# A one-layer hybrid trunk: the recurrent chain's operands kept as one DRAM record per chunk, causal mask and softmax normalisation moved

## The chip, the cores and the metric

The kernel runs on one core of a Trainium2 chip. The metric is device time in microseconds (us) of one execution. It is compared with a reference in float32.

## The reference, cut to what matters

One layer of a parallel-branch block works on T = 528 tokens (16 learned meta tokens ahead of 512) of width 1024. One input projection feeds a recurrent branch (RWKV-7, 8 heads of 64), an attention branch with forget gates (FoX, 8 heads of 64) and two sets of gates; the output of the meta tokens is dropped at the end.

```
u = rmsnorm(h);  proj = u @ w_in
# recurrent branch, per head, token by token:
sa = S a_t;  S = S * w_t + sa b_t + v_t k_t;  y_t = S r_t
y = groupnorm(y);  y_rw = (y + bonus) * g
# attention branch, per head, causal, in blocks of 128 queries:
logits = q k^T * scale + (F_q - F_k)
p = softmax(where(kpos <= qpos, logits, -inf));  y_fx = p v
# merge and MLP
h += (sig(gA) * (y_rw @ w_out_rw) + sig(gB) * (y_fx @ w_out_fx)) @ w_o
h += square(relu(rmsnorm(h) @ w_up)) @ w_down
```

## The kernel before, in words

**Features.** Every large product is made in three passes: each operand is split into a high and a low fp32r part, and hi-hi, lo-hi and hi-lo products are added up. The input projection (L468, tile `pj`) is 480 such weight blocks of 128x128, 1,440 matmuls: 24 feature jobs (12 for the recurrent branch, 12 for attention, each in two halves of 264 tokens) and 16 gate jobs of 512 tokens. Gates (`gt`) are stored to DRAM (`gd`, L491) and fetched again (`gl`, L1056) for the out projection.

**The recurrent branch** works in 4 pairs of heads (class `Pair`). For a pair, `decay` (L686; its first product is `pup`, L698) makes the decays, `keys` the keys (`BK` holds two key forms, L732), `rows` (L736) the decayed rows `L[e]` for each head e of the pair, in nine chunks of 64 tokens, `scores` (L763) the products of keys and rows (`psr`, L773) times a triangular mask. One head's products fill 128 partitions of PSUM, of which 64 go masked into `Bm` (L776) and 64 into the empty half of `L[e]` (L777), so that there are two multiplies for each of 24 PSUM tiles. `keys_turned` (L779) makes `bkT` (`pbt`, L788), `inverse` (L792) inverts the triangular matrices of a group of two pairs into `Tt`, and `chain` (L884) then steps through nine chunks for the group g = 0 or 1. A chunk is four dependent products: `pch` from `uv` and `L` (L911), a copy `Rs` (L913), `pch` from `Rs` and `Tt` (L917), two copies into `uv` (L919), the new state from `uv` and `bkT` (L932, L934), and the output `pyy` (L940, L943). The values of the next chunk are transposed inside the chain (`pvt`, L897) and copied into `uv` (L899). After chunks 4 and 8 `group_norm` (L951) normalises the output: DVE works out y (L954 to L963, with a Newton iteration for the reciprocal root, L221 to L228), PE transposes it (`pyt`, L970), adds the bonus `bv` and multiplies by the gate product `pg` (L977). All of this stays in SBUF: `L`, `Bm`, `bkT`, `ov` and `bv` are held for two pairs at a time. Pair 2 therefore waits for the first chain (`chained`, `normalised`, `values_read`, `inverted`) before it writes them.

**Attention** has 4 pairs with 4 query blocks i each (`attention`, L571): scores `psc` (L592), the causal mask added on DVE (L601), a fused add of the decay and running minimum (`pe`, `nm`, L603), an exponential with its sum on ACT (L606), a reciprocal (`rsum`, L607) and the division of the whole row by the sum on DVE (L608), transposes to `ppt`/`ppm` (L621, L623), copies (L625, L626), the product with the values `py` (L634, L637) in two 64-column halves of the array, one for each head, and a copy into `y_fx` (L638).

**What sets the order.** TensorE (PE) runs its instructions in the order in which they are written, and a planner writes them. `Clock` (L60) books an estimated duration for every instruction and keeps the time at which each tile is written and read. `Turns` (L150) has streams with a rank; it takes the stream of lowest rank whose next step is ready on the planner's clock with a margin (ROOM). Ranks: chain 0, recurrent 1, attention 2, attention's features 3, group norm 4, projections 8. So the projections are what fills PE between steps of the others. The other engines' instructions are sorted by a scheduler after the planner's urgency. All DMAs are issued in order by one queue, SP. PSUM has 8 banks: `pj` 2, the small products 4, `py` 1, `ch` 1.

After the mixer come the out projection (L1063) with the gates fetched again, merged on POOL (L1057, L1067), the product with w_o (L1095, L1112), a norm, and the MLP (L1146 up, L1179 down).

Of the kernel before, what the change touches and what calls it, by code (L numbers as in the profile page):

```python
# [12 lines left out]
I32 = mybir.dt.int32  # L13
# [46 lines left out]
class Clock:  # L60
# [13 lines left out]

    def last(self, name):
        return max(self.w.get(name, 0.0), self.r.get(name, 0.0))
# [6 lines left out]
    def ready(self, *aps):  # L83
        return max([self.w.get(a.tensor.name, 0.0) for a in aps] + [0.0])
# [11 lines left out]
    def read(self):  # L96
# [3 lines left out]
        for x in new:  # L100
# [10 lines left out]
            names = [a.tensor.name for a in ins]  # L111
# [5 lines left out]
            deps = max([self.w.get(n, 0.0) for n in names] + [self.free.get(out, 0.0)])  # L117
            if eng == "PE":
                n = max(cols(outs[0]), 64)
                big = tuple(x.tile_size) == (128, 128)  # L120
                if ins[0].dtype == F32R:
# [7 lines left out]
            else:  # L129
                size = max([cols(a) for a in outs + (ins if "Reduce" in str(x.opcode) else [])])  # L130
                if eng in self.RATE:
                    fixed, per = self.RATE[eng]

                    if eng == "DVE" and not any(a.tensor.space == PSUM for a in ins + outs):
                        fixed += 0.2
                    end = self.book(eng, max(deps, self.last(out)), fixed + per * size) + fixed + per * size
                else:
                    cost = 0.3 + size * 128 * 4 / 2.0e5
                    end = self.book("DMA", max(deps, self.last(out)), cost) + cost + 2.0
            for o in outs:  # L140
                self.w[o.tensor.name] = max(self.w.get(o.tensor.name, 0.0), end + self.HOP)
            for n in names:
                self.r[n] = max(self.r.get(n, 0.0), end + self.HOP)
# [6 lines left out]
class Turns:  # L150
# [4 lines left out]
    ROOM = {0: 0.0, 1: 0.8, 2: 1.5, 3: 1.5, 4: 2.5, 8: 0.5}  # L155
# [9 lines left out]
    def run(self):  # L165
        ck = self.clock
        while self.streams:
# [10 lines left out]
            ck.urgent = s[0] < 2  # L178
            with self.tc.high_priority() if ck.urgent else nullcontext():
# [8 lines left out]
def kernel(ctx, tc, ht, x, win, par, cst, gain, lora, wout, wo, wup, wdn, out, dbg=None):  # L188
# [15 lines left out]
    cs = cp.tile([128, 576], F32, name="cs")  # L204
    pr = cp.tile([128, N_PAR], F32, name="pr")
    ident, ones_blk, tmask, cmask = (cs[:, 128 * i:128 * i + 128] for i in range(4))
    mask16 = cs[:, 512:]
# [5 lines left out]
    qg8 = cp.tile([128, 1], F32, name="qg8")  # L213
    eps = cp.tile([128, 1], F32, name="eps")
    smask = cp.tile([128, NCH, 64], BF16, name="smask")

    def rsqrt(x, pool, tag, shape, iters=3):

        y = pool.tile(shape, F32, name=tag + "y", tag=tag + "y")
        w = pool.tile(shape, F32, name=tag + "w", tag=tag + "w")  # L220
        V.tensor_scalar(y.bitcast(I32), x.bitcast(I32), -0.5, float(0x5F3759DF), ALU.mult, ALU.add)  # L221
        c = 1.0
        for _ in range(iters):
            V.tensor_tensor(w, x, y, ALU.mult)
            V.tensor_tensor(w, w, y, ALU.mult)
            V.scalar_tensor_tensor(y, w, 3.0 * c * c, y, ALU.subtract, ALU.mult)
            c = -2.0 * c ** 3
        V.tensor_scalar(y, y, 1.0 / c, None, ALU.mult)  # L228
        return y
# [37 lines left out]
    yp = ctx.enter_context(tc.tile_pool(name="yp", bufs=1))  # L267
    gates_d = [dr.tile([128, S], F32, name=f"gd{i}") for i in range(16)]

    with ExitStack() as st:  # L270
# [38 lines left out]
        V.memset(eps, 1e-6)  # L309
        nc.scalar.preload_act_table_set("natural_log_exp_and_others")  # L310
# [7 lines left out]
        with tc.tile_pool(name="xp", bufs=2) as xp:  # L318
# [16 lines left out]
            nc.sync.dma_start(cs, cst)  # L335
# [3 lines left out]
            shifts = [tshift(12 + blk, lfs[i], name="tl", tag="ov", bufs=2) for i, blk in enumerate((B_LORA, B_GD))]  # L339
            for t in range(2):  # L340
# [28 lines left out]
                V.tensor_tensor(f0[:, tk], pf, rs[:8, tk], ALU.mult)  # L369
        y_rw = yp.tile([128, 4, S], F32, name="y_rw")  # L370
# [35 lines left out]
        for t_ in (lhi, llo):  # L406
            ck.w[t_.tensor.name] = 10.0
# [36 lines left out]
        def projections(total):  # L444
            fetched, done = None, 0
            while done < total:
# [5 lines left out]
                while cur is not None:  # L452
# [6 lines left out]
                    for a0, a1 in parts:  # L459
# [16 lines left out]
                        ck.urgent = rank < 2  # L476
                        if finish:
                            with tc.high_priority() if ck.urgent else nullcontext():
                                finish()
                        ck.read()  # L480
                        ck.urgent = False
# [18 lines left out]
        def fox_features():  # L500
            for p in range(4):
# [57 lines left out]
                vm = fp.tile([48, 128], F32, name="vm", bufs=2)  # L559
# [6 lines left out]
                for e, hs in enumerate(hss):  # L566
                    A.copy(vm[32 * e:32 * e + 16, hs], pvm[:16, hs])
# [3 lines left out]
        def attention():  # L571
            for p in range(4):
# [10 lines left out]
                def scored(i):  # L583
# [5 lines left out]
                    for a, b in parts:  # L589
                        for e, hs in enumerate(hss):  # L590
                            sc = psm("psc")[:, :b - a]
                            mm(sc, q[hs, 128 * i:128 * i + 128], k[hs, a:b], start=True, stop=True)  # L592
                            scs[e].append((sc, a, b))
                    pes = []
                    for e in range(2):
# [3 lines left out]
                        for x, (sc, a, b) in enumerate(scs[e]):  # L599
                            if b == n:  # L600
                                V.tensor_tensor(sc[:, b - a - 128:], sc[:, b - a - 128:], cmask, ALU.add)  # L601
# [3 lines left out]
                        rsum = fp.tile([128, 1], F32, name="rsum", bufs=3)  # L605
                        act(pe[:, :n], pe[:, :n], AF.Exp, bias=least, scale=-1.0, accum_out=rsum)  # L606
                        V.reciprocal(rsum, rsum)  # L607
                        V.tensor_scalar(pe[:, :n], pe[:, :n], rsum, None, ALU.mult)  # L608
                        pes.append(pe)
                    return pes  # L610

                def turned(i, pes):

                    pTs = []
                    pTm = fp.tile([48, 128], F32, name="pTm")
                    for e in range(2):
                        pe, m = pes[e], slice(32 * e, 32 * e + 16)
# [8 lines left out]
                        A.copy(pTm[m], ptm)  # L626
# [635 lines left out]
```

## Time and profile before

| | |
|---|---|
| median of 3 runs | 959.02 us (956.32 to 959.78) |
| the profiled execution | 958.41 us, its span 956.4 us |
| PE busy | 892.9 us, 93% of the span |
| DVE busy | 508.6 us, 53% |
| ACT busy | 438.9 us, 46% |
| POOL busy | 193.4 us, 20% |
| mean granted TensorE clock | 0.957 |
| DMA | 83.30 MB, mean 87 GB/s |

The times of one execution start at zero with the first instruction; 2.0 us of its time lie outside the span. In the views an instruction is named by its line, operation and tiles, output first ("pch<-uv,L"); "x8" means eight in a row taken together; brackets give the idle time of the engine ahead of it and the instruction that ended it. PEclk is the granted TensorE clock as a share of full speed. A float32 product that is not a transpose appears as two matmul records. SPq is the DMA queue's own sequencer.

### The profile page before, as it was taken

Reading aid. Unit: us, or ns where it says so; the run is one execution under the profiler, and the core shown is the slowest. Engines: PE = TensorE matmul, PEld = TensorE weight load, DVE = VectorE, ACT = ScalarE, POOL = GpSimd, SP = SyncE. Lnnn points to the kernel's source line nnn. Section 1 sums busy time; section 2 is a strip of 40 time slices with the busy share of each in tenths; the row PEclk is TensorE's granted clock in tenths of the full one; section 3 lists DMA queues with packets and bytes.
Section 4 is the critical chain, followed back from the end, with each engine's and each line's share of the span. In section 5 each row is a group of like instructions: output and inputs, shape, how many; then the busy total and the mean of one; then the engine's idle time right before and its main releaser. Section 6 shows DMA issues by size and latency. Waiting matters only on the chain.

```text
span 956.4 us, 15455 instructions
## 1 busy us (share of the span) xinstructions
PE 892.9 (93%) x5968; PEld 725.9 (76%) x5968; DVE 508.6 (53%) x1013; ACT 438.9 (46%) x899; POOL 193.4 (20%) x169
## 2 busy tenths in 40 slices
PE   7789998989979997999979799999999999999998
PEld 6667866758878765877558578988888888888886
DVE  6584677344767588354765655454523245543332
ACT  7745535675627545375644444343422224442221
POOL 1352643212524342421015510000000000000000
PEclk9887989999979999999979979999999999999999
DMA  5210213123101231311254452033333233333331
GB/s 200 86 59 24 67 56 108 36 67 100 48 30 49 67 103 48 111 35 46 67 169 150 157 158 72 2 108 91 97 99 99 92 96 99 100 99 93 116 121 56
DMA packets 45449, 83.30 MB, mean 87 GB/s; under 512 B 5048, under 2 KB 6200, under 8 KB 45376
## 3 DMA queue, kind: packets, MB, share of 16 engines
q1 hardware_dynamic: 45376, 82.32, 27.7%
q8 instruction: 47, 0.77, 0.3%
q14 instruction: 26, 0.21, 0.1%
HBM read 75.99 MB, written 6.31 MB: 86 GB/s over the span
## 4 chain that ended last, share of the span: by engine, by line
PE 62%; DVE 8%; ACT 5%; POOL 3%; DMA 2%; issue 1%; POOLq 0%; DVEq 0%; ACTq 0%; SPq 0%
PE po L1146 18%; PE pd L1179 18%; PE pj L468 11%; PE po L1095 2%; PE po L1112 2%; DMA gl<-gd 2%; POOL gl L1057 1%; PE py L637 1%; POOL gl L1067 1%; PE psc L592 1%; DVE tmp L824 1%; PE pw L842 1%; ACT L256 1%; PE ppt L623 1%; PE pch L917 1%
## 5 line engine op out<-in xcount | busy, mean ns | idle before, releaser
L238 DVE TENSOR_TENSOR wlo<-wraw,whi 128x512 fp32r<-128x512 f32 x152 | 109.4, 721 | 184.5 <-ACT whi L237 183.0
L237 ACT CAST whi<-wraw 128x512 fp32r<-128x512 f32 x152 | 94.0, 620 | 196.1 <-PE pd L1179 109.6
L468 PE MATMUL pj<-uhi,whi 128*128 128x264 f32 (+1 forms) x480 | 171.0, 356 | 0.2 <-ACT qa L519 0.2
L468 PE MATMUL pj<-uhi,wlo 128*128 128x264 f32 (+1 forms) x480 | 158.9, 331 | 0.5 <-POOL wlo L440 0.5
L468 PE MATMUL pj<-ulo,whi 128*128 128x264 f32 (+1 forms) x480 | 159.1, 331 | 0.0
L440 POOL TENSOR_TENSOR wlo<-wraw,whi 128x512 fp32r<-128x512 f32 x80 | 107.9, 1355 | 217.6 <-ACT whi L439 201.3
L468 PEld LDWEIGHTS pj<-uhi,whi 128*128 128x128 f32 x480 | 94.5, 197 | 20.5 <-issue 10.6
L468 PEld LDWEIGHTS pj<-uhi,wlo 128*128 128x128 f32 x480 | 94.8, 198 | 8.2 <-POOL wlo L440 0.7
L1179 PE MATMUL pd<-whi,fhi 128*128 128x512 f32 x256 | 99.6, 389 | 0.0
L1179 PE MATMUL pd<-wlo,fhi 128*128 128x512 f32 x256 | 99.6, 389 | 0.0
L1179 PE MATMUL pd<-whi,flo 128*128 128x512 f32 x256 | 99.6, 389 | 0.0
L468 PEld LDWEIGHTS pj<-ulo,whi 128*128 128x128 f32 x480 | 95.1, 198 | 4.8
L1146 PE MATMUL po<-zhi,whi 128*128 128x512 f32 (+1 forms) x248 | 94.8, 382 | 0.0
L1146 PE MATMUL po<-zlo,whi 128*128 128x512 f32 (+1 forms) x248 | 94.8, 382 | 0.0
L1146 PE MATMUL po<-zhi,wlo 128*128 128x512 f32 (+1 forms) x248 | 94.8, 382 | 0.0
L439 ACT CAST whi<-wraw 128x512 fp32r<-128x512 f32 x80 | 48.9, 617 | 44.6 <-PE pj L468 25.3
L1179 PEld LDWEIGHTS pd<-wlo,fhi 128*128 128x128 f32 x256 | 48.1, 188 | 10.0
L1179 PEld LDWEIGHTS pd<-whi,fhi 128*128 128x128 f32 x256 | 48.1, 188 | 9.9
L1179 PEld LDWEIGHTS pd<-whi,flo 128*128 128x128 f32 x256 | 48.1, 188 | 9.9
L1146 PEld LDWEIGHTS po<-zhi,wlo 128*128 128x128 f32 x248 | 46.6, 188 | 9.1
L1146 PEld LDWEIGHTS po<-zlo,whi 128*128 128x128 f32 x248 | 46.6, 188 | 9.1
L1146 PEld LDWEIGHTS po<-zhi,whi 128*128 128x128 f32 x248 | 46.6, 188 | 8.9
(303 smaller groups left out, 1509.5 us busy)
## 6 DMA issues: line engine op xcount, KB each, us to landing
wraw<-in_win SPq DMA_DIRECT2D x84, 256.0 KB, 2.8
wraw<-in_wup SPq DMA_DIRECT2D x64, 256.0 KB, 2.6
wraw<-in_wdn SPq DMA_DIRECT2D x64, 256.0 KB, 2.6
gd<-gt SPq DMA_DIRECT2D x16, 256.0 KB, 2.1
wraw<-in_wout SPq DMA_DIRECT2D x16, 256.0 KB, 2.8
gl<-gd SPq DMA_DIRECT2D x16, 256.0 KB, 3.0
wraw<-in_wo SPq DMA_DIRECT2D x16, 256.0 KB, 3.0
xt<-in_ht SPq DMA_DIRECT2D x8, 264.0 KB, 5.8
```

The lines of the kernel that those rows point to most:

```text
L237: A.copy(hi, raw)
L238: low.tensor_tensor(lo, raw, hi.bitcast(F32), ALU.subtract)
L256: p = nc.scalar.preload_act_table_set("natural_log_exp_and_others")
L439: A.copy(hi, raw)
L440: G.tensor_tensor(lo, raw, hi.bitcast(F32), ALU.subtract)
L468: mm(po, a, b[:, k, a0:a1], start=n == 0, stop=n == 23)
L592: mm(sc, q[hs, 128 * i:128 * i + 128], k[hs, a:b], start=True, stop=True)
L623: nc.tensor.transpose(pt[:, 128 * j:128 * j + 128], pe[:, NM + 128 * j:NM + 128 * j + 128], ident)
L1095: mm(pd[i], a[:, k, 128 * i:128 * i + 128], b, start=k == 0 and n == 0, stop=k == 7 and n == 2)
L1112: mm(po, a[:, k, 128 * i:128 * i + 128], b[:, k, :], start=n == 0, stop=n == 23)
L1146: mm(po[:, t0:t1], a, b[:, k, t0:t1], start=n == 0, stop=n == 23)
L1179: mm(pd[i], a[:, b_, 128 * i:128 * i + 128], b, start=b_ == 0 and n == 0, stop=b_ == 15 and n == 2)
```

## The change

**Records.** What the chain needs of a pair is written to DRAM, one record of 128x512 floats for each chunk: both heads' rows with their masked scores (columns 0 to 255), `bkT` (256 to 383), the second part of the masked scores (384 to 447) and `Tt` (448 to 511). `save` stores a part as soon as it is made. Values are transposed beforehand (`values_turned`) and stored in `vt_d`, the bonus in `bv_d`. The chain fetches two records and two halves of `uv` for the next chunk at the start of each one; `uv` has 2 buffers and `rec` 4. The waits of pair 2 for the first chain go, and only the second chain waits for the first one's last group norm.

**Scores and rows.** The masked scores of a head go with one multiply into one tile M[e]; rows for both heads are made together on 128 partitions.

**Attention.** The mask is added by a product of two bf16 tiles in PSUM. The exponentials are transposed and multiplied undivided; in `mixed` the exponentials are now the stationary operand, with all 128 columns, and the values the moving one; the result is scaled by the reciprocal sum on ACT, and transposed back on PE.

**Group norm** takes ln and exp on ACT for the reciprocal root. One of the two copies into `uv` (L919) is on ACT.

**Planner.** The clock keeps regions of tiles in place of whole tiles, and DMA costs by length of run. Ranks are now chain 0, attention 1, attention's features 2, recurrent 3.

```diff
-    ROOM = {0: 0.0, 1: 0.8, 2: 1.5, 3: 1.5, 4: 2.5, 8: 0.5}
+    AHEAD = {0: 100, 1: 40, 2: 20, 3: 20}
+    ROOM = {0: 0.0, 1: 1.0, 2: 1.5, 3: 1.0, 4: 2.5, 8: 0.5}
...
+    rec_d = [dr.tile([NCH, 128, 512], F32, name=f"rec{i}") for i in range(4)]
+    vt_d = [dr.tile([NCH, 64, 2, 2, 64], F32, name=f"vtd{i}") for i in range(2)]
+    bv_d = [dr.tile([128, S], F32, name=f"bvd{i}") for i in range(4)]
...
-                            mm(sc, q[hs, 128 * i:128 * i + 128], k[hs, a:b], start=True, stop=True)
+                            mm(sc, q[hs, 128 * i:128 * i + 128], k[hs, a:b], start=True, stop=b < n)
+                    for e in range(2):
+                        mm(scs[e][-1][0][:, b - a - 128:], masks[:, 0, :], masks[:, 1, :], start=False, stop=True)
...
-                            if b == n:
-                                V.tensor_tensor(sc[:, b - a - 128:], sc[:, b - a - 128:], cmask, ALU.add)
...
-                        V.tensor_scalar(pe[:, :n], pe[:, :n], rsum, None, ALU.mult)
...
-                    for j in range(i + 1):
-                        for e, hs in enumerate(hss):
-                            mm(py[hs], vt[:, j, hs], pTs[e][0][:, j, :], start=False, stop=j == i)
-                    A.copy(y_fx[:, p, 128 * i:128 * i + 128], py)
+                        mm(py[:, hs], pTs[e][1], vm[:, hs], start=True, stop=False)
+                        for j in range(i + 1):
+                            mm(py[:, hs], pTs[e][0][:, j, :], vt[:, j, hs], start=False, stop=j == i)
+                    yn = fp.tile([128, 128], F32, name="yn")
+                    for e, hs in enumerate(hss):
+                        act(yn[:, hs], py[:, hs], AF.Copy, scale=sums[e])
+                    yield lambda: max(ck.ready(yn), banks(1))
+                    pyT = psm("pyT")[:, :128]
+                    nc.tensor.transpose(pyT, yn, ident)
+                    A.copy(y_fx[:, p, 128 * i:128 * i + 128], pyT)
...
+            def save(self, rows, c0, c1, src):
+
+                nc.sync.dma_start(rec_d[self.p][:, rows, c0:c1].rearrange("c q x -> q c x"), src)
...
-                    for e, hs in enumerate(hss):
-                        os, sp = hss[1 - e], sps[e]
-                        V.tensor_tensor(Bm[hs, c0:c0 + 3, :], sp[hs, :3, :], bc(tmask[hs], 1, 3), ALU.mult)
-                        V.tensor_tensor(L[e][os, c0:c0 + 3, :], sp[os, :3, :], bc(tmask[os], 1, 3), ALU.mult)
+                    for e in range(2):
+                        V.tensor_tensor(M[e][:, c0:c0 + 3, :], sps[e][:, :3, :], bc(tmask, 1, 3), ALU.mult)
+
+                for e, hs in enumerate(hss):
+                    self.save(hss[1 - e], 128 * e, 128 * e + 128, M[e][hss[1 - e]])
+                    self.save(hs, 384, 448, M[e][hs, :, 64:])
...
+            def fetch_rec(c):
+                recs = []
+                for q in prs:
+                    t = rp.tile([128, 512], F32, name="rec", bufs=4)
+                    nc.sync.dma_start(t, rec_d[q.p][c])
+                    recs.append(t)
+                return recs
...
             for c in range(NCH):
-                yield lambda: ck.ready(uv)
+                nxt = None
+                if c < NCH - 1:
+                    nxt, nxt_recs = new_uv(c + 1), fetch_rec(c + 1)
+                yield lambda: ck.ready(uv, *recs)
...
-                for e, hs in enumerate(hss):
-                    V.tensor_copy(uv[hs, 0, e], ch[hs, 1])
+                for e, (hs, copy) in enumerate(zip(hss, (V.tensor_copy, A.copy))):
+                    copy(uv[hs, 0, e], ch[hs, 1])
...
-            rs = rsqrt(st2, rp, "rsg", [128, 2, 4])
-            V.tensor_tensor(y, y, bc(rs, 3, 64), ALU.mult)
+            after(act(st2, st2, AF.Ln, bias=epsg, scale=1.0 / 64), pinned(s_))
+            act(st2, st2, AF.Exp, scale=-0.5)
+            V.tensor_tensor(y, y, bc(st2, 3, 64), ALU.mult)
...
-        turns.add(1, recurrent())
-        turns.add(2, attention())
-        turns.add(3, fox_features())
+        turns.add(3, recurrent())
+        turns.add(1, attention())
+        turns.add(2, fox_features())
```

How the order moves is shown at three places. The first is PE near the end of the mixer. Before, this is what stands behind the last projection matmul (`pj`); the streams named are the second chain (`pch`), attention of pair 3 (`ppt`) and the group norm (`pyt`, `pg`).

```order
L468 MATMUL pj<-uhi,wlo 128x512
L917 MATMUL pch<-Rs,Tt 64x64 x4
L897 MATMUL pvt<-cs,ov 64x128 x2
L621 MATMUL ppt<-cs,pe 16x128
L623 MATMUL ppt<-cs,pe 128x128
L970 MATMUL pyt<-cs,y_rw 64x128 x4
L977 MATMUL pg<-lhi,lw_4541 128x256
L977 MATMUL pg<-llo,lw_4541 128x256
L977 MATMUL pg<-lhi,lw_4542 128x256
L932 MATMUL pch<-uv,bkT 64x64 x4
```

And this is what stands around the last projection matmul now.

```order
L653 MATMUL ppt<-cs,pe 16x128
L655 MATMUL ppt<-cs,pe 128x128 x3
L500 MATMUL pj<-uhi,whi 128x512
L500 MATMUL pj<-ulo,whi 128x512
L500 MATMUL pj<-uhi,wlo 128x512
L1021 MATMUL pyt<-cs,y_rw 64x128 x4
L1028 MATMUL pg<-lhi,lw_4667 128x256
L1028 MATMUL pg<-llo,lw_4667 128x256
L1028 MATMUL pg<-lhi,lw_4668 128x256
L625 MATMUL psc<-ka,qa 128x272 x2
L625 MATMUL psc<-ka,qa 128x256 x2
```

Before, the whole last chunk of the chain and query blocks 1 to 3 of pair 3 stand behind the last `pj`; now the chain has ended ahead of it, and of attention only the scores of query block 3 and what follows them stand behind it. The number of `pj` matmuls is the same, 1,440. From the first to the last chunk's first product the first chain had 189 of them before and has 63 now (the place of 36 of the former is taken by steps of pair 2 and of attention); the second chain had 132 and has 102. At the start of PE's order 36 `pj` stood ahead of the first `pup`, and 78 do now.

The second place is the DMA queue SP while the first chain runs. Before, it holds weights (`wraw`, `lraw`) and a gate's store.

```order
L658 DMA lraw<-in_lora 128x128 [waits DVE_49,PE_49]
L430 DMA wraw<-in_win 128x512 [waits DMAHW3_49,Pool_49]
L658 DMA lraw<-in_lora 128x128 [waits DMAHW2_49,DMAHW0_49,DVE_49]
L430 DMA wraw<-in_win 128x512 [waits DMAHW7_49]
L491 DMA gd_77<-gt 128x512 [waits Activation_49]
L658 DMA lraw<-in_lora 128x128 [waits DMAHW5_49,DMAHW2_49,DVE_49]
L430 DMA wraw<-in_win 128x512 [waits DMAHW6_49,Pool_49]
```

Now the chain's fetches stand in it: `rec` is a pair's record, `uv` the values, `vtd` their store; `rec_77<-M` is a save of pair 2.

```order
L940 DMA rec<-rec_75 128x512 [waits DMAHW4_49,PE_49]
L948 DMA uv<-vtd_79 64x2x128 [waits DMAHW5_49,DMAHW6_49,PE_49,Activation_49]
L948 DMA uv<-vtd_79 64x2x128
L940 DMA rec<-rec_76 128x512 [waits DMAHW7_49]
L462 DMA wraw<-in_win 128x512 [waits DMAHW0_49]
L521 DMA gd_90<-gt 128x512 [waits DMAHW1_49,Activation_49]
L802 DMA rec_77<-M_2569 64x9x128 [waits DMAHW2_49,DVE_49]
L948 DMA uv<-vtd_79 64x2x128 [waits DMAHW3_49,PE_49]
```

Each chunk has four fetches, the first of which wait for PE (the products that read the buffers two chunks back), and a gate's store and a save stand among them. The whole queue holds 452 rows in place of 309.

The third place is SP where the out projection begins. Before, the residual `hres` stands ahead of the gates `gl`:

```order
L234 DMA wraw<-in_wout 128x512 [waits DMAHW2_49,DVE_49,Activation_49]
L1076 DMA hres<-in_x 128x1024 [waits DVE_49,PE_49,Activation_49]
L1076 DMA hres<-in_x 128x1024 x3
L1056 DMA gl_5588<-gd_75 128x512 [waits DVE_49,PE_49,DMAHW3_49,Activation_49,Pool_49]
L1056 DMA gl_5606<-gd_83 128x512 [waits DMAHW4_49]
```

Now the gates come first:

```order
L256 DMA wraw<-in_wout 128x512 [waits DMAHW6_49,DVE_49,Activation_49]
L1097 DMA gl_5719<-gd_85 128x512 [waits DMAHW0_49,DVE_49,Activation_49]
L1097 DMA gl_5737<-gd_93 128x512
L1097 DMA gl_5770<-gd_86 128x512
L1097 DMA gl_5788<-gd_94 128x512 [waits DMAHW7_49]
```

The first `gl` waited for PE and POOL before, and does not wait for them now.

More of the change, by code (lines that the diff above doesn't have):

```diff
@@ L135, in read @@
                         fixed += 0.2
-                    end = self.book(eng, max(deps, self.last(out)), fixed + per * size) + fixed + per * size
+                    end = self.book(eng, deps, fixed + per * size) + fixed + per * size
                 else:
[L138 to L143, printed above, removed]
+                    run = min(self.run(a) for a in outs + ins)
+                    cost = 0.1 + 4 * math.prod(n for _, n in outs[0].ap) / (1.2e5 if run < 128 else 2.0e5 if run < 512 else 3.3e5)
+                    end = self.book("DMA", deps, cost) + cost + 2.0
+            for g in go:
+                self.note(self.w, *g, end + self.HOP)
+            for g in gi:
+                self.note(self.r, *g, end + self.HOP)
 class Event:
@@ L475, in projections @@
                         ck.read()
[L476 removed]
+                        ck.urgent = False
                         if finish:
[L478 removed]
+                            with tc.high_priority(20) if rank < 9 else nullcontext():
                                 finish()
[L480 to L481 removed]
                     ev.done = True
@@ L840, in six @@
                 for n in range(b0, b0 + 6):
-                    for hs in hss:
-                        mm(ps_[hs, n - b0, :], lhs(n)[hs], rhs(n)[hs], start=True, stop=True)
-                return ps_
-            def now(t):
-                ck.read()
-                return ck.ready(t)
-            at = now(Dn)
-            w2_at, d_at, w_at = [], [], []
+                    for e, hs in enumerate(hss):
+                        mm(ps_[hs, n - b0, :], lhs(n, e)[hs], rhs(n)[hs], start=True, stop=True)
@@ new lines, in recurrent @@
+            for p, q in enumerate(pairs):
+                g, j = divmod(p, 2)
+                yield from q.decay()
+                yield q.k_in
+                yield from q.keys()
+                done = Event()
+                if j == 0:
+                    pairs[p + 1].ask_keys(done)
+                yield q.r_in
+                q.rows()
+                done.done = True
+                yield from q.scores()
+                yield from q.keys_turned()
+                yield q.v_in
+                yield from q.values_turned()
+                yield from q.bonus()
+                if p < 3:
+                    pairs[p + 1].ask_values()
+                if j == 1:
+                    if g == 0:
+                        pairs[2].ask_keys()
+                    yield from inverse(g, pairs[p - 1:p + 1])
+                    turns.add(0, chain(g, pairs[p - 1:p + 1]))
```

270 lines of the change are left out of this document (131 added, 139 removed).

## The prediction

> **What bounds the kernel now.** I read the busy times by stage first. Columns: window, its length, busy time of PE, PE's weight loads, DVE, ACT and POOL with their instructions, granted clock, DMA share, GB/s.
>
> ```profile
> 28.00:464.00 436.00, 398.67 (x3598) 320.50 (x3598) 268.37 (x596) 239.59 (x531) 153.29 (x134) 0.94 0.20 61
> 464.00:497.00 33.00, 24.36 (x194) 16.84 (x194) 26.49 (x85) 17.63 (x49) 0.00 (x0) 0.76 0.38 128
> 602.00:956.00 354.00, 350.38 (x1617) 292.83 (x1615) 138.44 (x205) 113.04 (x190) 0.00 (x0) 1.00 0.31 93
> ```
>
> The MLP (602 on) keeps PE busy for 350.4 of 354 us at full clock, and no edit touches it. The change lies in the mixer, 28 to 497. PE is busy there for 398.7 + 24.4 = 423 of 469 us, so 46 us are idle; and the clock, 0.94 over 436 us and 0.76 over 33, costs up to 26 + 8 = 34 us more, as far as PE worked meanwhile. Everything that the change can win is in these 80 us. Next, who ends PE's idle time in the mixer: total us, times, longest.
>
> ```profile
> PE psr L773 <- DVE L L777: 7.4, 4, 4.2
> PE pup L698 <- ACT lhi L261: 5.9, 1, 5.9
> PE psr L773 <- DVE BK L732: 5.6, 2, 3.8
> PE ppt L621 <- DVE rsum L607: 5.5, 1, 5.5
> PE pyt L970 <- DVE y_rw L963: 4.7, 1, 4.7
> ...
> PE ppm L621 <- DVE pe L608: 2.3, 1, 2.3
> PE psr L773 <- DVE nm L603: 2.2, 1, 2.2
> ```
>
> These seven are 33.6 of the 46 us: DVE late with the masked scores and with the softmax, a group norm, and one stall at the start. None is a DMA. The clock I read in three stretches of 10 us:
>
> ```profile
> 70.00:80.00 10.00, 9.90 (x48) 7.58 (x46) 6.67 (x14) 3.56 (x6) 2.49 (x2) 0.50 0.19 52
> 120.00:130.00 10.00, 8.37 (x41) 6.62 (x41) 8.53 (x15) 1.44 (x4) 4.17 (x5) 0.66 0.18 54
> 270.00:280.00 10.00, 7.75 (x40) 6.93 (x41) 9.53 (x26) 0.54 (x2) 0.20 (x1) 0.50 0.08 28
> ```
>
> The clock falls to half behind a long wait and stays there for some 10 us: a stall costs about its length again.
>
> **The end of the mixer.** Start, time over the row's matmuls, and in brackets PE's wait:
>
> ```profile
> 463.57 0.40 PE L468 MATMUL pj<-uhi,wlo 128*128 128x512 f32 x1
> ...
> 470.47 0.45 PE L943 MATMUL pyy<-uv,Bm 64*64 64x64 f32 x8
> ...
> 481.75 1.03 PE L970 MATMUL pyt<-cs,y_rw 128*64 128x128 f32 x4 [4.72 <-DVE y_rw L963]
> ...
> 485.60 1.59 PE L592 MATMUL psc<-ka,qa 64*128 64x272 f32 x6
> ...
> 488.36 0.88 PE L637 MATMUL py<-pT,vt 128*64 128x128 f32 x12
> 491.54 0.38 PE L621 MATMUL ppm<-cs,pe 128*16 128x128 f32 x1 [2.31 <-DVE pe L608]
> ...
> 497.08 0.80 PE L1063 MATMUL po<-yhi,whi 128*128 128x512 f32 x1 [0.36 <-ACT y_fx L638]
> ```
>
> The last filler ends near 464, the chain at 470.9. The 26.2 us from there to the out projection (497.1) hold the window's 8.6 us of idle time (33 - 24.4); of the other 17.6, some 7 are lost to the clock (33 x 0.24 = 8 in the window from 464), which leaves 10.6 of work at full clock. So 15.6 us are lost.
>
> **The change part by part**, against the profiled execution's 958.41 us (2.0 us outside its span of 956.4), which is 0.6 us under the median.
>
> *1. End.* By the new order 33 more projection matmuls stand beside attention's blocks 0 to 2 and the chain has ended before the last of them. Bare are only the scores of block 3 with what follows, the piece from 485.60 to 497.08, 11.5 us, of which by the same share (10.6 of 26.2, a little more because its rows are dense) 5.2 are work. The division (L608) goes from that path, but a scaling on ACT, a transpose and one more copy come in, so I leave 11.5. That is 6.3 us lost in place of 15.6: **-9** (0 to -13).
>
> *2. Start.*
>
> ```profile
> 31.78 0.28 PE L468 MATMUL pj<-uhi,wlo 128*128 128x264 f32 x1
> 37.96 0.59 PE L698 MATMUL pup<-lhi,lw 64*128 64x264 f32 x2 [5.89 <-ACT lhi L261]
> ```
>
> Now 78 `pj` stand ahead of this product and not 36. The 42 more take 42 x 0.12 = 5.0 us (the rows ahead of 31.78 follow each other at 0.12), nearly all of the wait: **-5** (-3 to -6). If ACT is later than now, behind the table load and copy that it has there in the new order, the rest remains.
>
> *3. DVE's waits.* What DVE loses, us in all and mean ns:
>
> ```profile
> L608 DVE TENSOR_SCALAR pe<-pe,rsum 128x144 f32<-128x144 f32 (+3 forms) x32 | 15.0, 474 | 0.6
> ...
> L776 DVE TENSOR_TENSOR Bm<-psr,cs 64x384 f32<-64x384 f32 x24 | 13.2, 549 | 0.8 <-PE psr L773 0.6
> L777 DVE TENSOR_TENSOR L<-psr,cs 64x384 f32<-64x384 f32 x24 | 13.1, 554 | 0.4
> ...
> L743 DVE TENSOR_SCALAR L<-okk 64x9 f32<-64x9 f32 x8 | 9.0, 1128 | 0.0
> L601 DVE TENSOR_TENSOR psc<-psc,cs 128x128 f32<-128x128 f32 x32 | 8.9, 294 | 5.1 <-PE psc L592 5.0
> ```
>
> L608 and L601 go (23.9), one of each pair L776/L777 goes (13.1), L743 is halved (4.5): 41 of DVE's 268.4 + 26.5 = 295 us, without the smaller ones. In the score waits a bank comes free after one multiply of 0.55 us and not two; in the softmax waits 0.47 + 0.29 us go for each head. These waits (7.4 + 5.6 + 2.2 + 5.5 + 2.3 = 23.0) should about halve: **-12** (-4 to -18). `BK` (5.6) gets no faster itself, only less queued.
>
> *4. Clock.* Of the 26 us in 28 to 464, the stretches behind waits of 3.8 us and more are what (2) and (3) can mend. I take two of some 5 us each, 10 us at 0.50: **-10** (-3 to -20).
>
> The Trainium skill, "TensorE: Matmul & The Clock Gate", section "Part 1: The HAM clock gate", has the array at half rate after at least one idle window of about 3.4 us and at full rate after one busy window. By that rule waits that merely shrink below 3.4 us would already save their whole stretch, and the term would be -15 and the sum 935. The stretch 120 to 130, at 0.66, speaks against so sharp an edge, since no wait near it is long:
>
> ```profile
> 116.12 0.46 PE L773 MATMUL psr<-L,BK 64*128 64x128 f32 x2 [1.75 <-DVE BK L732]
> 120.47 0.46 PE L773 MATMUL psr<-L,BK 64*128 64x128 f32 x2 [1.21 <-DVE L L777]
> 122.09 1.10 PE L773 MATMUL psr<-L,BK 64*128 64x128 f32 x10 [1.16 <-DVE L L777]
> ```
>
> Several waits of 1.2 to 1.8 us within 8 us are enough here. So I stay with -10.
>
> *5. More work on PE.* The old `py` products use two 64-column halves side by side: at 488.36 twelve records start within 0.88 - 0.27 us, 0.055 each. On the whole array the nearest row is a 128x128 product with 128 weight columns:
>
> ```profile
> 458.06 0.60 PE L562 MATMUL pv<-cs,vf 128*128 128x128 f32 x4
> ```
>
> Here four start within 0.60 - 0.27 us, 0.109 each. The new `mixed` has 112 products in 224 records: 224 x (0.109 - 0.055) = 12.1. The 32 mask products are bf16 and unseen: 0.05 to 0.11 each, 2.6 in the middle; 16 transposes at 0.109 make 1.7. Fewer changes between halves and whole array give back some 2. Sum **+14** (+8 to +20). PE is the bound wherever filler stands, so this counts in full.
>
> *6. Fetches of the chain.* Now 72 DMAs stand on its path, in order on SP. The nearest rows (KB, then us to landing) and the chain's period:
>
> ```profile
> gd<-gt SPq DMA_DIRECT2D x16, 256.0 KB, 2.1
> ...
> gl<-gd SPq DMA_DIRECT2D x16, 256.0 KB, 3.0
> ```
>
> ```profile
> 496.87 1.75 SPq L1056 DMA_DIRECT2D gl<-gd  x4
> ```
>
> ```profile
> 443.21 0.45 PE L911 MATMUL pch<-uv,L 128*64 128x64 f32 x8
> ...
> 447.32 0.45 PE L943 MATMUL pyy<-uv,Bm 64*64 64x64 f32 x8
> ...
> 449.37 0.45 PE L911 MATMUL pch<-uv,L 128*64 128x64 f32 x8
> ```
>
> Four issues take 1.75 us and the last lands 3.0 later: 4.7 us. They may start when the chunk before has read its buffers, at 447.8, and are needed two chunks after 443.21, at 2 x 6.16 = 455.5: 7.7 us of room, if SP is free. At the start of a chain `Tt` must be stored and fetched, 2.1 + 3.0 + issues, twice, partly beside filler. I take **+6** (0 to +40, a rival below).
>
> *7.* The gates no longer wait for PE and POOL, behind 1.75 us of `hres`: **-2** (-4 to +3). Nothing else is put on a path: the stores and ln/exp with their table loads lie on queues and an ACT that is 257 of 469 us busy (239.6 + 17.6).
>
> Sum: -9 - 5 - 12 - 10 + 14 + 6 - 2 = -18: 958.4 - 18 = **940 us**.
>
> **The rivals.** *No change.* Filler is only moved: the projection matmuls are as many, and the first chain has 63 of them around its chunks in place of 189. What stands there instead (pair 2 and attention) itself waits for DVE. If each of the 18 chunks then shows 1 us, less than one of the waits at 116 and 120, the 18 us are paid back: 953 to 963. For it speaks that waits come from short dependent steps; against it, that DVE has 41 us less to do.
>
> *Slower: fetches behind others on SP.* In this queue a DMA that waits for its data holds all behind it. Before, such waits cost nothing, since PE never waited for a DMA:
>
> ```profile
> SPq L491 <- ACT gt L490: 86.6, 12, 19.5
> ...
> SPq L580 <- DVE nm L603: 44.5, 2, 26.2
> ```
>
> Now stores of gates and of pair 2's scores, and `nF`, stand between the chain's fetches. PE is in order too, so a late record stops all streams. Without term 6 the sum is -24; over 16 chunks the gain is gone at 1.5 us each and the kernel is slower by 0.5% at (24 + 4.8) / 16 = 1.8. At 2.4 it is 958.4 - 24 + 38 = 973. Against it stand 7.7 us of room for 4.7.
>
> *Larger gain.* The DVE waits go wholly (-23), the clock term is -20, the end -13, the start -5.9, and no fetch is late: with +14 and -2 that is -50, 908. For it speaks that the rank of the recurrent steps is now behind attention, so that they should find their data ready.
>
> **How the numbers follow.** A measurement of this kernel tells about 0.5% (4.8 us) from no change. I give the forecast's case (-35 to -5) 0.55, the larger gain 0.15, no change 0.10, slower 0.20. So faster 0.70, same 0.10, slower 0.20. The range, 912 to 966, leaves out about half of the larger gain (0.08) and 0.12 of the slower case.
>
> **What would show it.** Right: the wait of `pup` at 38 us under 2 us; waits of `psr` and `ppt` on DVE about 11 us in all; projection matmuls until about 12 us before the out projection; a mean clock in the mixer above 0.95; records of the new `py` 0.11 us apart. Wrong: waits of `pch` or `pyy` ended by a DMA of `rec` or `uv`, more than 1.5 us a chunk, would make it the slower case; a tail as long as now, or DVE waits of 20 us and more in the first chain, no change.

## The result, and the profile after

The changed kernel takes 930.84 us (median of 4 runs, 929.3 to 932.28), the kernel before 957.67 us beside it. The ratio is 0.9724, with a 95% interval of 0.9686 to 0.9763: 2.8% faster. The forecast was 940 us, 912 to 966. The profiled execution after took 930.17 us with a span of 928.4, against 958.41 and 956.4.

The same windows of the mixer after (columns as before: window, length, busy PE, PEld, DVE, ACT, POOL, clock, DMA share, GB/s); the mixer now ends at 467.8, where the out projection starts, and not at 497.1:

```profile
28.00:452.47 424.47, 402.22 (x3756) 327.58 (x3755) 226.09 (x483) 252.84 (x582) 152.93 (x136) 0.98 0.42 120
452.47:467.82 15.35, 11.83 (x86) 9.20 (x85) 8.78 (x25) 9.63 (x28) 0.00 (x0) 1.00 0.50 154
```

The mixer is 439.8 us long and was 469.1. PE is idle in it for 25.8 us (439.82 - 414.06) and was for 46.0; the clock loses 0.02 of 424 us, 8.5, and lost 34. DVE is busy for 234.9 us and was for 294.9. Idle time and clock gave 20.2 + 25.5 = 45.7 us by these rounded shares, the mixer got 29.3 shorter, so by this estimate some 16 us of work came to PE. The out projection takes 1.5 us longer, and the MLP is as long as before.

Who ends PE's idle time in the mixer now:

```profile
PE pch L970 <- DVE Rs L966: 4.4, 1, 4.4
PE pup L735 <- ACT lhi L283: 2.9, 1, 2.9
PE pch L982 <- ACT uv L972: 2.9, 4, 1.3
PE pj L500 <- ACT vf L579: 2.8, 1, 2.8
PE po L1104 <- ACT yhi L283: 2.3, 1, 2.3
PE pyT L674 <- ACT yn L671: 2.0, 2, 1.4
PE ppt L655 <- ACT fsq L565: 1.8, 1, 1.8
PE py L666 <- DVE nm L636: 1.4, 1, 1.4
PE psr L826 <- DVE BK L769: 1.2, 1, 1.2
...
PE pch L964 <- DMA rec<-rec: 0.2, 1, 0.2
```

The waits of the score products (`psr`) and of the softmax for DVE, 23.0 us before, are down to under 3. What is left is one wait of 4.4 us for `Rs` and many short ones, a good half of the time on ACT. The chain waits for a record once, for 0.2 us.

The end of the mixer in the timeline of PE, from the last projection matmul:

```profile
452.08 0.39 PE L500 MATMUL pj<-uhi,wlo 128*128 128x512 f32 x1
...
453.19 1.33 PE L625 MATMUL psc<-ka,qa 64*128 64x272 f32 x6
...
461.66 1.06 PE L668 MATMUL py<-vt,pT 128*128 128x64 f32 x8
...
464.44 0.33 PE L674 MATMUL pyT<-cs,yn 128*128 128x128 f32 x1 [0.61 <-ACT yn L671]
464.61 0.60 PE L1021 MATMUL pyt<-cs,y_rw 128*64 128x128 f32 x4
...
467.82 0.79 PE L1104 MATMUL po<-yhi,whi 128*128 128x512 f32 x1 [2.26 <-ACT yhi L283]
```

From 452.5 on 15.4 us are left, of which 11.8 are work at full clock. Before, 26.2 us were left behind filler and chain, with 15.6 lost.

### The profile page after: what moved, and what is told of

It is laid out like the page before. It is cut to its first block, busy times and chain, and to the rows that moved or that the text cites. A ratio compares the mean times of both kernels' runs of the same rounds, so it can differ in the third digit from the quotient of the medians.

```text
span 928.4 us, 15700 instructions
## 1 busy us (share of the span) xinstructions
PE 883.4 (95%) x6016; PEld 724.3 (78%) x6016; DVE 455.9 (49%) x850; ACT 446.7 (48%) x933; POOL 194.3 (21%) x170
## 4 chain that ended last, share of the span: by engine, by line
PE 43%; POOL 2%; DVE 2%; DMA 2%; issue 1%; ACT 0%; POOLq 0%; DVEq 0%
PE po L1187 19%; PE pd L1220 19%; PE po L1136 2%; PE po L1153 2%; DMA gl<-gd 2%; POOL gl L1108 1%; POOL gl L1098 1%; DVE ylo L284 1%; PE pd L1169 0%; DVE mlo L1110 0%; DVE gl L1106 0%; ACT mhi L1109 0%; DVE we L284 0%; ACT gl L1099 0%; PE po L1104 0%
## 5 line engine op out<-in xcount | busy, mean ns | idle before, releaser
L500 PE MATMUL pj<-uhi,whi 128*128 128x264 f32 (+1 forms) x480 | 167.2, 348 | 3.0 <-ACT vf L579 2.8
L472 POOL TENSOR_TENSOR wlo<-wraw,whi 128x512 fp32r<-128x512 f32 x80 | 111.7, 1402 | 220.1 <-ACT whi L471 191.6
L500 PE MATMUL pj<-uhi,wlo 128*128 128x264 f32 (+1 forms) x480 | 155.6, 324 | 0.0
L500 PE MATMUL pj<-ulo,whi 128*128 128x264 f32 (+1 forms) x480 | 155.2, 323 | 0.0
L500 PEld LDWEIGHTS pj<-uhi,whi 128*128 128x128 f32 x480 | 91.5, 191 | 17.6 <-issue 5.5
L500 PEld LDWEIGHTS pj<-uhi,wlo 128*128 128x128 f32 x480 | 91.2, 190 | 7.5 <-POOL wlo L472 0.2
L500 PEld LDWEIGHTS pj<-ulo,whi 128*128 128x128 f32 x480 | 91.7, 191 | 4.0
```

The lines of the kernel that those rows point to most:

```text
L472: G.tensor_tensor(lo, raw, hi.bitcast(F32), ALU.subtract)
L500: mm(po, a, b[:, k, a0:a1], start=n == 0, stop=n == 23)
```

## The experiments

Two theories were set against each other. **Relief**: the time came from DVE having 60 us less to do, so that PE waits less for it. **Order**: it came from steps being free to stand elsewhere (pair 2 beside the first chain, attention ahead of the recurrent steps), so that filler and independent steps cover the waits to the end. In the forecast the first carried -12 and most of the clock's -10, the second -9.

All runs, with their profile's mixer (from 28 us to the first out projection matmul), PE's idle time and mean clock in it. Beside the runs the kernel before took 957.21 to 959.78 us, so rows are better compared by their ratios than by their medians:

| run | median us | ratio to before (95%) | mixer us | idle us | clock |
|---|---|---|---|---|---|
| before | 957.67 | | 469.1 | 46.0 | 0.92 |
| changed | 930.84 | 0.9724 (0.9686 to 0.9763) | 439.8 | 25.8 | 0.98 |
| old ranks | 960.91 | 1.0030 (1.0004 to 1.0055) | 471.5 | 43.0 | 0.93 |
| new ranks in the kernel before | 964.38 | 1.0074 (1.0043 to 1.0105) | 482.8 | 53.4 | 0.90 |
| pair 2 waits | 946.40 | 0.9857 (0.9819 to 0.9895) | 458.7 | 36.1 | 0.96 |
| old attention | 931.86 | 0.9703 (0.9662 to 0.9745) | 444.2 | 36.7 | 0.95 |
| old attention, pair 3 a stream of its own | 925.06 | 0.9650 (0.9629 to 0.9672) | 432.9 | 31.3 | 0.98 |
| the same with pairs 2 and 3 | 925.42 | 0.9665 (0.9648 to 0.9681) | 435.1 | 29.1 | 0.98 |
| changed attention, pair 3 a stream of its own | 928.13 | 0.9690 (0.9669 to 0.9711) | 440.1 | 26.1 | 0.98 |
| old softmax, new mask | 929.79 | 0.9700 (0.9679 to 0.9720) | 439.1 | 26.3 | 0.96 |
| the same, pair 3 a stream of its own | 928.90 | 0.9699 (0.9677 to 0.9721) | 441.1 | 29.0 | 0.96 |
| two multiplies per score | 936.26 | 0.9772 (0.9748 to 0.9797) | 449.7 | 27.1 | 0.96 |
| late fetch | 930.54 | 0.9704 (0.9674 to 0.9735) | 439.3 | 27.1 | 0.99 |
| every record fetched twice | 942.60 | 0.9826 (0.9802 to 0.9851) | 452.6 | 36.1 | 0.98 |

Every edit goes through the planner, which places the instructions anew. No run changes a cost and leaves the rest of the order exactly as it was.

**The old ranks in the changed kernel.**

```diff
-        turns.add(3, recurrent())
-        turns.add(1, attention())
-        turns.add(2, fox_features())
+        turns.add(1, recurrent())
+        turns.add(2, attention())
+        turns.add(3, fox_features())
```

> The changed kernel with the old ranks of the planner's streams (recurrent 1, attention 2, its features 3); all else as changed. Relief theory (the gain is TensorE's shorter waits for VectorE, whose work was cut): the waits stay short, 929 to 937 us. Order theory (the gain is the freedom to put steps where filler is, which the ranks steer): attention falls to the end again, with idle time and half clock there, 940 to 952 us.

Measured: 960.91 us. The whole gain is gone, further than the order theory said. PE's longest waits in the mixer are then:

```profile
PE pj L500 <- ACT whi L471: 12.3, 2, 6.4
PE pch L970 <- DVE Rs L966: 5.3, 3, 3.9
PE pj L500 <- POOL wlo L472: 5.2, 6, 1.8
```

The waits of `psr` for DVE stay away, so the relief is there all the same. But projections wait for their converted weights (17.5 us; ahead of the longest such wait, which ends at 103, ACT is busy for 8.9 of the 9 us from 94, about half of it with table loads of 1.28 us each), and attention of pair 3 stands bare at the end, at a clock of 0.67:

```profile
468.16:499.45 31.29, 24.17 (x125) 17.20 (x123) 15.11 (x45) 14.76 (x48) 1.52 (x1) 0.67 0.28 100
```

Less work on DVE, together with the other edits, is worth nothing in this order. PE's added work is among them, so the relief by itself is not priced here.

**The new ranks in the kernel before.** The same edit the other way round, with the new margins, and without records or the new attention.

> The kernel before with only the new ranks and margins of the planner (attention 1, its features 2, recurrent 3); no records, old attention. If the ranks alone make the gain: 930 to 945 us. If they need the records (pair 2 must be able to go on beside the first chain): the second inversion and the whole second chain stand behind the last projection, some 50 us of steps without filler at half clock, 975 to 1000 us.

Measured: 964.38 us, 0.7% slower than before; neither number was met, but the sign is that of the second case. The profiled execution, at 974.3 us 10 us above the median, shows the second chain behind the last projection (441.18), as expected, with PE at half clock:

```profile
450.00:460.00 10.00, 8.95 (x78) 7.10 (x76) 5.68 (x16) 4.18 (x13) 0.00 (x0) 0.50 0.17 59
460.00:470.00 10.00, 8.49 (x98) 5.96 (x97) 3.18 (x11) 4.96 (x17) 0.00 (x0) 0.50 0.01 2
470.00:480.00 10.00, 8.55 (x94) 5.82 (x90) 4.65 (x15) 4.53 (x15) 0.00 (x0) 0.50 0.01 2
480.00:490.00 10.00, 6.81 (x68) 5.01 (x67) 5.82 (x23) 4.15 (x12) 0.00 (x0) 0.50 0.00 0
```

So the ranks alone lose 0.7%, all the other edits without the ranks lose 0.3%, and both together win 2.8%. Each needs the other. The runs below take single edits out; the planner's changed clock, the group norm and the second engine for the copies into `uv` were not tried by themselves, so what they contribute is open.

**Pair 2 waits for the first chain again.** Records and ranks stay.

```diff
                 yield q.r_in
+                if p == 2:
+                    yield chained[0]
                 q.rows()
```

> The changed kernel in which pair 2 waits for the end of the first chain before it makes its rows, as before; the records stay. Relief theory: the planner fills with projections, 930 to 936 us. Order theory (pair 2 beside the first chain is what leaves filler for the end): the tail is bare again for 10 to 20 us more, 941 to 955 us.

Measured: 946.40 us, in the middle of what the order theory expected: 16 us of the 27 go by the medians, 13 by the ratios. The place is another. The tail is hardly longer (17.4 us after the last projection against 15.4), but the last projection stands at 468.9 in place of 452.1:

```profile
28.00:469.29 441.29, 411.78 (x3758) 335.45 (x3756) 229.64 (x481) 256.91 (x584) 151.81 (x136) 0.96 0.41 116
469.29:486.69 17.40, 10.78 (x86) 9.29 (x86) 10.44 (x27) 11.37 (x31) 0.00 (x0) 0.91 0.42 136
```

Ahead of it PE is idle for 29.5 us against 22.3, and the clock is 0.96 against 0.98: the loss lies in the middle of the mixer, not at its end as the order theory had it.

**The old attention**: mask and division on DVE, values stationary, no transposes back.

```diff
+                            if b == n:
+                                V.tensor_tensor(sc[:, b - a - 128:], sc[:, b - a - 128:], masks[:, 1, :], ALU.add)
...
+                        V.tensor_scalar(pe[:, :n], pe[:, :n], rsum, None, ALU.mult)
...
-                        mm(py[:, hs], pTs[e][1], vm[:, hs], start=True, stop=False)
+                        mm(py[hs], vm[32 * e:32 * e + 16, hs], pTs[e][1], start=True, stop=False)
```

> The changed kernel with the old attention: causal mask and division on VectorE, values stationary in two halves of the array, no mask products and no transposes back. VectorE gets about 24 us more work, TensorE some 16 us less. Relief theory: waits for VectorE come back by more than the 16 us saved, 935 to 948 us. Order theory: VectorE has room (half idle), so the saved TensorE work shows, 917 to 925 us.

Measured: 931.86 us, as fast as the changed kernel; neither theory had it. Its mixer falls into two parts:

```profile
28.00:434.95 406.95, 386.00 (x3551) 309.78 (x3552) 242.55 (x529) 237.48 (x531) 150.08 (x131) 0.99 0.41 118
434.95:472.23 37.28, 21.55 (x244) 17.09 (x244) 17.74 (x43) 18.72 (x50) 0.00 (x0) 0.59 0.46 147
```

To 435 it is 17 us ahead of the changed kernel's last projection, and then six chunks of the second chain stand bare at a clock of 0.59. The first part is shorter by the saved work on PE, but also because more is left for the second (244 matmul records against 86 behind the changed kernel's last projection); there the gain is lost.

**Old attention, pair 3 as a stream of its own behind the recurrent one.** If that is so, something has to be kept back for the second chain.

```diff
-        turns.add(1, attention())
+        turns.add(1, attention(range(3)))
+        turns.add(4, attention([3]))
```

> The old attention (mask and division on VectorE) in the changed kernel, and attention of pair 3 as a stream of its own with a rank behind the recurrent one (4), so that it is left to fill the second chain. The old attention alone took 931.9 us with the second chain bare for some 30 us. Order theory: the bare end goes to under 15 us and the 16 us of TensorE work saved show, 912 to 922 us. If something else holds it (VectorE's waits): 928 to 936 us.

Measured: 925.06 us, faster than both kernels (0.965, 0.9629 to 0.9672, against 0.9724, 0.9686 to 0.9763, for the changed one, each to the kernel before beside it). The bare end is halved:

```profile
442.61:460.88 18.27, 8.47 (x103) 7.02 (x103) 9.55 (x21) 9.46 (x22) 0.00 (x0) 0.81 0.48 149
```

It is still 18 us, 7.5 of them one wait for the last group norm (`pyt` for `y_rw`), which is more than the 3 us by which the range of 912 to 922 was missed. With pairs 2 and 3 behind:

```diff
-        turns.add(1, attention(range(3)))
-        turns.add(4, attention([3]))
+        turns.add(1, attention(range(2)))
+        turns.add(4, attention([2, 3]))
```

> The old attention with the streams split after pair 1: pairs 2 and 3 at rank 4, behind the recurrent stream. By its order the second chain has ended before the last projection, and only the last query blocks and group norms stand behind it. Order theory: a bare end as short as in the changed kernel with 16 us less TensorE work, 914 to 922 us. If late attention waits for VectorE beside the chain: 925 to 935 us.

Measured: 925.42 us. The chain's end is covered, as its order said, but waits of attention for DVE and a longer wait for the split of y (`yhi`, 3.9 us) stand there instead. This is the second of the two cases expected.

**The changed attention with that stream**, to price the new attention with streams alike: the edit that gives pair 3 rank 4, on the changed kernel.

> The changed attention with the pair-3 stream of its own at rank 4: beside the run that has the old attention with the same streams (925.1 us) it prices the changed attention on TensorE. If TensorE's added work (some 14 to 16 us) counts in full: 936 to 942 us. If VectorE's 24 us less give it back: 922 to 930 us.

Measured: 928.13 us, in the second range and 3 us above the old attention. Both mixers in one row each, the changed attention first:

```profile
28.00:468.10 440.10, 414.03 (x3843) 337.32 (x3841) 234.73 (x508) 262.85 (x611) 153.68 (x137) 0.98 0.42 122
```

```profile
28.00:460.88 432.88, 401.62 (x3794) 320.90 (x3792) 258.70 (x572) 255.78 (x580) 150.15 (x131) 0.98 0.43 123
```

PE is busy for 12.4 us longer, DVE for 24.0 us less, at the same clock. PE's idle time is 5.2 us shorter; how much of this is relief is open, since in the run with the old attention a single wait for a group norm is 7.5 us. With these streams the new attention is no gain. That it is a loss is at the edge of the noise, since the two intervals meet (up to 0.9672, from 0.9669), and with the streams left as they were there is no difference (931.86 against 930.84 us).

**Old softmax and product, new mask**, without and with the stream of its own: the diff of the old attention without its first two lines, on the changed kernel.

> The changed kernel with division on VectorE and the old product (values stationary, two halves); the mask stays a product on TensorE. 15 us more for VectorE, 13 to 14 us less for TensorE. By its order only group norms and the last two query blocks stand behind the last projection, as in the changed kernel. Order theory (TensorE's work counts, VectorE has room): 915 to 922 us. Relief theory: 931 to 940 us.

> Division on VectorE and the old product, mask by TensorE, attention of pair 3 as a stream of its own at rank 4. With the mask on VectorE too this took 925.1 us, with the whole changed attention 928.1 us. If the masks' TensorE time (32 products of some 0.1 us) is what differs: 927 to 929 us. If VectorE's 9 us less for masks matter more: 920 to 924 us.

Measured: 929.79 and 928.90 us. Both miss the lower range. The first lies just under its upper one and has its idle time at 26.3 us like the changed kernel, and its clock at 0.96 and not 0.98; the second falls in its first case, 3.8 us above the old mask. That the 32 mask products make these 3.8 us is not shown: the order differs too.

**Two multiplies for each masked score.**

```diff
                     for e in range(2):
-                        V.tensor_tensor(M[e][:, c0:c0 + 3, :], sps[e][:, :3, :], bc(tmask, 1, 3), ALU.mult)
+                        for hs in hss:
+                            V.tensor_tensor(M[e][hs, c0:c0 + 3, :], sps[e][hs, :3, :], bc(tmask[hs], 1, 3), ALU.mult)
```

> The changed kernel with each masked score made by two multiplies on 64 partitions again, 48 in place of 24, some 13 us more for VectorE. Relief theory: the waits of the score products for VectorE, about 10 us less now than before, come back with their half clock, 940 to 950 us. Order theory: 929 to 934 us, score waits under 3 us in all.

Measured: 936.26 us, 5.4 above the changed kernel and between the two ranges. The score waits did not come back:

```profile
PE psr L826 <- DVE tm L317: 1.8, 1, 1.8
PE psr L826 <- DVE BK L769: 1.3, 1, 1.3
PE psr L826 <- ACT BK L770: 0.2, 1, 0.2
```

Idle time is 27.1 us, 1.3 more than in the changed kernel. The rest is clock (0.96) with a new order. DVE is busy for 16.5 us longer (251.3 against 234.9). So 16 us of DVE work cost some 5 us, at the edge of the noise (0.9748 to 0.9797 against 0.9686 to 0.9763), by a way that the relief theory does not name.

**Late fetch**: the next chunk's records are fetched at the end of a chunk.

```diff
-                    nxt, nxt_recs = new_uv(c + 1), fetch_rec(c + 1)
+                    nxt = new_uv(c + 1)
...
-                    uv, recs = nxt, nxt_recs
+                    uv, recs = nxt, fetch_rec(c + 1)
```

> The changed kernel with the two records of the next chunk fetched at the end of a chunk and not at its start. If the fetches have room enough (their issue waits for buffers anyway, and the planner fills the gap) 930 to 938 us, with waits of the chain for a record under 1 us each. If a late record stops TensorE as the slower rival has it, 16 chunks by 2 to 3 us: 960 to 980 us.

Measured: 930.54 us, no difference; the chain waits for a record once, for 0.3 us. The transfers have room in an order that is planned around them.

**Every record fetched twice** into the same buffer, the second load behind the first one's landing.

```diff
-                    nc.sync.dma_start(t, rec_d[q.p][c])
+                    for _ in range(2):
+                        nc.sync.dma_start(t, rec_d[q.p][c])
```

> The changed kernel in which every record is loaded twice into the same buffer, the second load behind the first one's landing in the same queue: 36 loads more, about 3 us more to each record. If fetches have room (7.7 us for 4.7 by the forecast's rows, and filler ahead of the chunk): 930 to 937 us, waits for a record under 3 us in all. If the slower rival's price is real once the room is used up (its 1.8 us a chunk and more): 955 to 985 us, with waits of the chain for a record of 2 to 4 us at most chunks.

Measured: 942.60 us, 11.8 us above the changed kernel, between the two ranges. The waits for records are 3.4 us in all, six of them, none over 0.9:

```profile
PE pj L500 <- ACT vf L579: 5.4, 1, 5.4
...
PE pch L965 <- DMA rec<-rec: 3.4, 6, 0.9
```

The waits of 2 to 4 us did not come, because the planner books the loads and moves the chunks apart: from the first to the last chunk's first product the first chain takes 78 us (213.2 to 291.1) and took 57 (209.1 to 266.3). PE's idle time is 10.3 us longer than in the changed kernel: 3.2 of it wait for records, 2.6 for `vf` (5.4 against 2.8). Where the rest arises was not settled. So fetches do cost time once their room is used up, 0.7 us a chunk (11.8 over 16). The slower rival's way, PE stopped by a late record, is 3.4 of the 11.8 us; the rest goes with the new order.

## Why the prediction was right, and where it was not

The sign and the range held; the gain was 27 us where 18 were forecast. The terms:

1. *End, -9.* Right, somewhat more: 3.5 us are lost now (15.4 less 11.8) in place of 15.6, so -12. The piece behind the last projection is 15.4 us and not 11.5, but it runs at full clock. The reason held too: with the old ranks the bare end is 31.3 us.
2. *Start, -5.* The wait of `pup` is 2.9 us and a second one 0.75; before they were 5.9 and 0.2. That is -2.5: the 42 matmuls moved ahead gave their 5 us, but ACT delivered later (the product starts at 40.3 us and not at 38.0), the case that the term named.
3. *DVE's waits, -12.* These waits fell by 20 us, more than the half that was assumed. (Of the 23.0 us the 2.3 for `pe` lie in the end too and were counted in both terms.) But this is where the reasoning failed: the step took the waits to fall because DVE has less to do. With the old ranks DVE has as little to do, these waits are as short, and 961 us remain, since idle time appears in other places. In the changed kernel four waits on ACT and DVE (`Rs`, `uv`, `vf`, `yn`) make 12.1 us, where the first two made 4.4 before and the others were not there, so that all idle time fell by no more than these waits did (20.2 us), although the waits of `pup` and of the group norm shrank as well. What the runs put in its place: less work on DVE, with the edits that come with it, pays only in an order that does not open waits elsewhere (961 us without it, 931 with it).
4. *Clock, -10.* It gave 17.7 us outside the end by the rounded shares (26.2 less 8.5); the case of -20 was nearer. Cut where the clock changes, the mixer now has four stretches at half clock:

```profile
41.20:44.60 3.40, 3.15 (x18) 2.91 (x19) 2.56 (x4) 2.64 (x6) 2.85 (x4) 0.50 0.29 81
160.60:164.00 3.40, 3.09 (x11) 2.39 (x12) 0.78 (x2) 3.35 (x8) 0.08 (x1) 0.51 0.24 77
215.30:218.70 3.40, 3.40 (x25) 2.15 (x21) 2.11 (x7) 1.84 (x6) 2.44 (x6) 0.50 0.79 174
338.10:341.50 3.40, 3.40 (x10) 2.62 (x9) 1.55 (x3) 1.59 (x5) 3.20 (x3) 0.51 0.15 44
```

Ahead of them stand waits of 2.9, 1.8, 4.4 and 2.8 us. The kernel before had 54.6 us at half clock ahead of its end, in six stretches of 3.4 to 17 us, so that half of the difference to 13.6, 20.5 us, is the gain by this count. The Trainium skill ("TensorE: Matmul & The Clock Gate", "Part 1: The HAM clock gate") has half rate after at least one idle window of about 3.4 us. The prediction's -15 by that rule was nearer than its -10, but three of the four waits are shorter than 3.4 us, and the last section shows half clock on a busy PE, which the rule does not give.
5. *Work on PE, +14.* Right: PE's balance gives some 16 (19 if the half clock is counted by stretches), and with streams alike the new attention has 12.4 us more busy time. The product's records follow each other at (1.06 - 0.27) / 7 = 0.113 us (461.66), against 0.109 assumed.
6. *Fetches, +6.* Too high: 0.2 us of waiting. The room that the rows gave (4.7 us needed of 7.7) was enough, and the doubt about a queue held up by others did not come true.
7. *Gates, -2.* Wrong sign, small: the out projection takes 1.5 us more. It starts at half clock (0.76 over its first 7.2 us), behind a wait of 2.3 us for the split of y on ACT, which still belongs to the mixer; and its waits for the gates (`gl`) are 3.2 us where they were 2.8.

That the sum came within 9 us is in part luck. The terms for DVE's waits, the clock and the fetches gave too little gain, by some 8, 8 to 10 and 6 us; the waits that opened in other places (some 8 us) were in no term, and with the start, the gates and the work on PE they took much of that back. Of the signs named, the clock above 0.95 and records 0.11 us apart came; `pup` waits longer than 2 us, `psr` and `ppt` shorter than 11, and the projections end 15 us ahead of the out projection and not 12.

The rival "no change", given 0.10, was the one to take more seriously: with the old ranks the kernel is no faster. Its mechanism, some 1 us shown at each of the 18 chunks, is a part of it at most: PE's waits in the chain's `pch` are 7.8 us there, and 7.7 us in the changed kernel, where they were 3.8 before. The larger gain came near on the end (-12 of -13), on the old waits for DVE (-20 of -23) and on the clock; it failed on the start (-2.5 of -5.9) and on the waits that took the place of the old ones.

## What to carry to other kernels

Where one engine is the bound and independent work fills its waits, a shorter wait and cheaper work on another engine are worth only what the order can use: try the order (ranks, waits that hold back a whole group) with each part by itself before crediting the part. Look at what stands behind the last piece of filler; keep work that is not on the long dependent chain back for it, as the stream of pair 3 does. Moving work from an engine with room to the bound engine, as the new attention does, costs about what it adds, less the idle time that it saves (here 12.4 less 5.2 us of the mixer).

## What the runs showed of the hardware

**Half clock on a busy PE.** In the kernel before with the new ranks PE stands at 0.50 from 450 to 490 us although it is busy for 6.8 to 9.0 of each 10 us, with small products in a dependent chain. Its waits from 450 to 500 us, all of them:

```profile
PE pch L917 <- DVE Rs L913: 3.9, 9, 0.8
PE pyt L970 <- DVE y_rw L963: 2.7, 1, 2.7
PE ppm L621 <- DVE pe L608: 0.7, 1, 0.7
```

No wait is longer than 2.7 us. Nor did a wait bring the clock down: it fell at 449.0, and from 425 to 450 us PE waited once, for 0.2 us.

```profile
445.60:449.00 3.40, 3.13 (x67) 2.00 (x61) 1.94 (x7) 3.28 (x9) 0.00 (x0) 1.00 0.56 177
449.00:452.40 3.40, 3.22 (x26) 2.10 (x25) 2.23 (x10) 2.88 (x8) 0.00 (x0) 0.50 0.40 119
452.40:496.80 44.40, 36.90 (x364) 27.14 (x364) 20.72 (x68) 19.06 (x61) 0.00 (x0) 0.50 0.03 10
```

From 443 to 447 us stand products of 32x32, ahead of the fall; the clock was at 1.00 again after 496.8, 48 us later. In the changed kernel the end of the mixer, 77% busy with larger products, ran at 1.00. That the size of the products decides is a guess; no run varied it alone.

**One instruction, two durations.** The masked scores on 128 partitions take as long as on 64 (549 ns before), so that half as many multiplies take half the time:

```profile
L828 DVE TENSOR_TENSOR M<-psr,cs 128x384 f32<-128x384 f32 x24 | 12.5, 552 | 13.0 <-PE psr L826 12.9
```

The product of the decayed rows, from SBUF to SBUF, takes twice as long in the mean, 1542 ns on 128 partitions in place of 751 on 64, and nothing was saved. But that mean mixes two durations. Here are minimum, median and maximum in ns before, in the changed kernel and with the old ranks:

```profile
L744 DVE TENSOR_TENSOR L<-orr,P x8: 740/750/757, 55.5 to 301.1; 64x576 f32<-64x576 f32 x8
```

```profile
L779 DVE TENSOR_TENSOR Lf<-orr,P x4: 753/1774/1867, 50.4 to 290.2; 128x576 f32<-128x576 f32 x4
```

```profile
L779 DVE TENSOR_TENSOR Lf<-orr,P x4: 741/744/1811, 49.9 to 283.4; 128x576 f32<-128x576 f32 x4
```

One of the four in the changed kernel, and three of the four with the old ranks, take as long as on 64 partitions. So the number of partitions is not what doubles the time. POOL was at work beside all the slow ones of these two runs, but beside quick ones too; what makes the difference was not tried.
